# How the low parts of the up weights are made in a one-core decoder-layer kernel

## The chip, the core and the metric

The kernel runs on one core of a Trainium2 chip, as one program from its first load to its last store. The metric is the device time of one execution in microseconds (us), and less is better. Beside the time there is a profile of one execution: which instruction ran on which engine, from when to when, and what the DMA queues moved. The names of the engines in it are PE for the matrix unit (TensorE; PEld is its loading of weights), DVE for VectorE, ACT for ScalarE, POOL for GpSimd and SP for SyncE; a "q" behind a name (SPq) is that engine's sequencer, which issues DMAs.

## What is computed

One decoder layer for 256 tokens of width 2048, in float32. Its first half mixes tokens (pooling, attention over latents, attention over a memory); its second half, on which the change bears, is a gated feed-forward network with 5632 inner columns:

```python
def conv_glu_ffn(h, w_gate, w_up, conv_w, conv_b, w_down):
    S = h.shape[1]
    g = h @ w_gate
    gp = jnp.pad(g, ((0, 0), (CONV_WIDTH - 1, 0), (0, 0)))
    gc = conv_b
    for j in range(CONV_WIDTH):
        gc = gc + conv_w[j] * gp[:, j:j + S]
    return (jax.nn.silu(gc) * (h @ w_up)) @ w_down
```

## The kernel before

**Two parts of every number.** The matrix unit is fed in a shorter form of float32 (F32R). To keep the precision, every operand is split: the high part is the number rounded to that form, and the low part is the number minus its high part. A product is then high weight by both parts of the activation, plus low weight by the high part of the activation. Activations lie as 512 columns: 256 high, then 256 low. So `gemm_t` issues for each 128 x 128 weight tile one matmul of 512 columns with the high part (line 104) and one of 256 columns with the low part (line 107). All activations of the feed-forward are kept in SBUF; only weights are streamed.

**How weights come in.** `load_w` (line 78) takes a 1 MiB block of weights (128 partitions by 2048 numbers) from memory into one of three `wr` tiles, with a DMA on SP's queue (line 81). `split_w` (line 84) works on half of such a block, 1024 columns: ScalarE copies it, rounded, into a `wh` tile (line 90), and VectorE subtracts that from the raw half into a `wl` tile (line 91). There are three `wh` and three `wl` tiles. Thus a `wh` tile can be written again when the eight matmuls of line 104 that read it are done, a `wl` tile when the eight of line 107 are done, and a `wr` tile can be loaded again when both halves have been copied and subtracted.

**The loop around the change.** The feed-forward first runs 44 times over blocks of 128 inner columns (line 631). One pass loads a block of gate weights and a block of up weights, and multiplies each with all 16 tiles of `h2`: four half blocks in a row on the matrix unit, here called G0, G1 (gate) and U0, U1 (up). Each half is eight matmuls of line 104 followed by eight of line 107. Behind the products stand small steps on ScalarE and VectorE: `scaled` (lines 623 to 629) for gate and up, the convolution (lines 640 and 642), the silu (line 643), their product (line 645) and the split of the result into `aT` (lines 128 and 129). Then 16 passes over the down weights follow (line 648), with the same `load_w` and `gemm_t`. The pool `fp` that holds `aT` and the small tiles of this stage is opened behind the mixing stage and takes the place of that stage's tiles (lines 617 to 621).

**What sets the order.** The kernel is written as a sequence of tile operations. A scheduler orders them for each engine by their place in the program and by when it reckons them ready, and it adds every wait. Each engine then executes its own list strictly in that order, so an instruction that waits holds up all those behind it on its engine. On ScalarE the copies of line 90 run three halves ahead of the matrix unit, and between them stand the small steps of the pass before.

GpSimd has no part in the feed-forward before the change; SP issues the weight loads and the stores of the output.

Of the kernel before, what the change touches and what calls it, by code (L numbers as in the profile page):

```python
# [18 lines left out]
P = 128  # L19
# [30 lines left out]
NVEC = _o  # L50
# per-token tables: cos | sin (each NT x 32), rope gains of q | k (64 each), pool edge factors (4 x 16)
TAB = {"cos": (0, NT * 32), "sin": (64, NT * 32), "gq": (128, 64), "gk": (192, 64), "edge": (256, 64)}
# [4 lines left out]
def layer(ctx, tc, xT_d, memT_d, vec_d, tab_d, w_z_d, w_mqkr_d, w_q_d, w_kv_d, w_mem_d, w_pool_d, w_o_d,  # L57
# [26 lines left out]
    def split_w(raw, o, n, cut=HS):  # L84
        """high and low parts of raw[:, o:o + n]"""
        hi = stage.tile([P, HS], F32R, tag="wh", name=nm("wh"), bufs=3)
        lo = stage.tile([P, HS], F32R, tag="wl", name=nm("wl"), bufs=3)
        for c in range(0, n, cut):
            e = min(n, c + cut)
            nc.scalar.copy(hi[:, c:e], raw[:, o + c:o + e])  # L90
            nc.vector.tensor_tensor(lo[:, c:e], raw[:, o + c:o + e], hi[:, c:e].bitcast(F32), op=ALU.subtract)  # L91
        return hi, lo

    def gemm_t(ps, raw, o, act, ks, first=True, last=True):
        """ps[:, :256] + ps[:, 256:] (+)= W[ks].T @ act(ks); W columns on partitions, tokens free.
        Tile i of W is raw[:, o + i * 128:]; act(k) has the parts of the activations of tile k."""
        ks = list(ks)
        nk = HS // P
        for c in range(0, len(ks), nk):
            kc = ks[c:c + nk]  # L100
            hi, lo = split_w(raw, o + c * P, len(kc) * P)
            end = last and c + nk >= len(ks)
            for i, k in enumerate(kc):
                nc.tensor.matmul(ps[:, :2 * T], hi[:, i * P:(i + 1) * P], act(k), start=first and c + i == 0,  # L104
                                 stop=False, skip_group_check=True)
            for i, k in enumerate(kc):
                nc.tensor.matmul(ps[:, T:2 * T], lo[:, i * P:(i + 1) * P], act(k)[:, 0:T], start=False,  # L107
                                 stop=end and i == len(kc) - 1, skip_group_check=True)

    def gemm_n(pss, hi, lo, act, k0, first, last):  # L110
        """pss[tt][j] (+)= act[:, k0:, tile tt].T @ W[:, :, span j]; tokens on partitions. hi/lo: [P, k, n]"""
        nk, n = hi.shape[1], hi.shape[2]
# [12 lines left out]
    def split_act(dst, src, scale=None):  # L125
        """dst[:, :T], dst[:, T:] = high and low parts of src (times a per-partition scale)."""
        if scale is None:
            nc.scalar.copy(dst[:, 0:T], src)
            nc.vector.tensor_tensor(dst[:, T:2 * T], src, dst[:, 0:T].bitcast(F32), op=ALU.subtract)
        else:  # L130
            nc.scalar.activation(dst[:, 0:T], src, AF.Copy, scale=scale)  # L131
            nc.vector.scalar_tensor_tensor(dst[:, T:2 * T], src, scale, dst[:, 0:T].bitcast(F32),  # L132
                                           op0=ALU.mult, op1=ALU.subtract)

# [1 line left out]
    vec = const.tile([P, NVEC], F32, name="vec")  # L136
# [14 lines left out]

    # the tensor engine's clock is raised, and the activation tables are loaded, while the first loads are on their way
    warm = const.tile([P, 1], F32, name="warm")
# [5 lines left out]
    def rsqrt_(dst, src, scale):  # L159
        """dst = (src * scale + eps) ** -0.5"""  # L160
        nc.scalar.activation(dst, src, AF.Sqrt, bias=eps[:], scale=scale)
        nc.vector.reciprocal(dst, dst)
# [19 lines left out]
    class SumSq:  # L182
        """sum over tiles and partitions of squares, per token"""

# [18 lines left out]
    def col_sums(ps, src):  # L203
        """ps[:, tt] = sum over partitions of src[:, tile tt]"""
        for tt in range(NT):
            nc.tensor.matmul(ps[:, tt:tt + 1], src[:, tt * P:(tt + 1) * P], ones[:, 0:1], start=True, stop=True)

    def head_sq(dst, src):
        """dst[:, h] = sum over the last dim of src[:, h, :]^2"""
        sq = mp.tile([P, 512], F32, tag="hsq", name=nm("hsq"), bufs=2)  # L210
# [4 lines left out]
    def to_features(dst, src, tt, n, scale=None, eng=None):  # L215
        """dst[:, i, tile tt] = src[:, i * 128:].T (times a per-partition scale), i < n <= 4"""
        ps = ps_aux()
# [10 lines left out]

# [1 line left out]
    mg = big.tile([P, KD, 2 * T], F32R, tag="act", name="mg")  # L230
# [9 lines left out]

# [1 line left out]
    mv = mp.tile([P, NT, XH, XD], F32, name="mv")  # L242
# [54 lines left out]
    mem_kv(0)  # L297
# [1 line left out]
    tab = mp.tile([P, NTAB], F32, name="tab")  # L299
    nc.sync.dma_start(tab[:], tab_d)  # L300
    # combined gains of the two sides of a score, and gained rotation tables
    gqk = mp.tile([P, 2], F32, name="gqk")
# [16 lines left out]

# [1 line left out]
    xs = SumSq()  # L321
# [12 lines left out]

# [1 line left out]
    NH = 288  # L336
# [22 lines left out]

# [1 line left out]
    def softmax_pv(ps, spans, f, v_of, dst):  # L361
        """ps: scores of each query tile at spans, keys in tiles of P; dst gets the parts of the output's transpose"""
        p = mp.tile([P, 512], F32, tag="p", name=nm("p"), bufs=2)
# [9 lines left out]
        for i, (a, b) in enumerate(spans):  # L373
            nc.vector.tensor_scalar(p[:, a:b], p[:, a:b], st[:, 6 + i:7 + i], None, op0=ALU.mult)
        # turned: for each key tile, the query tiles that see it
        tp = ps_aux()
# [24 lines left out]
    def half_add(dst, ps):  # L401
        """dst = ps[:, :T] + ps[:, T:]"""
        t = mp.tile([P, T], F32, tag="hadd", name=nm("hadd"), bufs=3)
        nc.scalar.copy(t[:], ps[:, 0:T])
        nc.vector.tensor_tensor(dst, t[:], ps[:, T:2 * T], op=ALU.add)

# [1 line left out]
    zl = mp.tile([P, 6, 2 * T], F32R, name="zl")  # L408
# [16 lines left out]

    # scale of the normalised latents, per token: s = rx * (rx^2 mean(z^2) + eps)^-0.5
    sl, sl2 = sm(4), sm(4)
# [10 lines left out]

# [1 line left out]
    zp = mp.tile([P, 4, T], F32, name="zp")  # L440
# [6 lines left out]

# [1 line left out]
    def pool_mix():  # L449
# [16 lines left out]

# [1 line left out]
    qkv = big.tile([P, 32, T], F32, tag="act", name="qkv")  # L468
# [6 lines left out]
    def rotate(dst, src, s, tt, nh):  # L475
        """dst = rotated src [P, nh, 64] with the gained tables of side s"""
        x1, x2 = src[:, :, 0:32], src[:, :, 32:64]
# [29 lines left out]

# [1 line left out]
    # keys are scaled by f_k = ((s_kv^2 |kn|^2 + rx^2 |kr|^2) / QK + eps)^-0.5 and turned  # L509
    sskr, fk, fkn, fkr = sm(NT), sm(NT * H), sm(NT * H), sm(NT * H)  # L510
# [30 lines left out]

# [1 line left out]
    pool_in(0)  # L543
# [8 lines left out]
    q_up(1)  # L552
    # f_q = s_q (s_q^2 mean + eps)^-0.5 / sqrt(QK), applied as the softmax scale
    fq = sm(NT * H)
# [15 lines left out]

# [1 line left out]
    def mla(h):  # L572
# [10 lines left out]
    def out_half(i, m):  # L583
        """x (+)= the part i of the output projection, for the pair of feature tiles m, m + 1"""
        raw = load_w(w_o_d[i][m // 2], STG)
# [13 lines left out]

# [1 line left out]
    h2 = big.tile([P, KD, 2 * T], F32R, tag="act", name="h2")  # L601
# [16 lines left out]

# [1 line left out]
    fp = ctx.enter_context(tc.tile_pool(name="ffn", bufs=1))  # L620
    aT = fp.tile([P, KF, 2 * T], F32R, name="aT")

    def scaled(ps, tag):
        """(ps[:, :T] + ps[:, T:]) * rstd"""
        t = fp.tile([P, T], F32, tag=tag, name=nm(tag), bufs=2)
# [5 lines left out]
    for f in range(KF):  # L631
# [4 lines left out]
        psu = ps_main()  # L636
        gemm_t(psu, raw, 0, lambda k: h2[:, k, :], range(KD))
        g = scaled(psg, "g")
# [21 lines left out]
def _pack(**i):  # L660
# [3 lines left out]
    def cols(w):  # L664
        """[k*128, m*128] -> [m, 128, k*128]: one block of columns per tile, rows on partitions"""
        k, m = w.shape[0] // P, w.shape[1] // P
        return np.ascontiguousarray(w.reshape(k, P, m, P).transpose(2, 1, 0, 3)).reshape(m, P, k * P)

    def rows(w, nk):
        """[k*128, n] -> [k/nk, 128, nk*n]: nk row tiles per block"""  # L670
        k, n = w.shape[0] // P, w.shape[1]
# [67 lines left out]
```

## Time and profile before

| | us |
|---|---|
| median of 3 runs | 1044.78 |
| lowest and highest of them | 1044.51 and 1045.87 |
| span of the profiled execution, first to last instruction | 1043.6 |
| of it: PE busy | 1034.8 |
| DVE busy | 708.8 |
| ACT busy | 542.5 |
| POOL busy | 1.5 |

The profiled execution has no time of its own beside its span; the runs lie 0.9 to 2.3 us above that span, which is what an execution has around it and from run to run. An engine's busy time is the sum of the durations of its instructions; it doesn't tell whether the engine set the time. That is read from a stage: which wait ends last there.

### The profile page before, as it was taken

What the parts mean: (1) busy time and instruction counts of PE and PEld (TensorE: products, weight loads), DVE (VectorE), ACT (ScalarE), POOL (GpSimd) and SP (SyncE); (2) the same over time, 40 slices, a digit from 0 to 9 for tenths busy, and PEclk for the clock granted to TensorE, in tenths of its full rate; (3) what the DMA queues carried; (4) which work ended last, traced back from release to release, by engine and by line L of the source; (5) the groups of instructions that cost most, each with busy time, mean ns of one, the idle gap of its engine ahead of it and who ended that gap; (6) DMA issues with size and microseconds to landing.
All of it is one profiled execution on the core that took longest, in us unless ns stands there. A gap on an engine that the chain in (4) does not pass through costs nothing.

```text
span 1043.6 us, 14921 instructions
## 1 busy us (share of the span) xinstructions
PE 1034.8 (99%) x5852; PEld 897.2 (86%) x5852; DVE 708.8 (68%) x1141; ACT 542.5 (52%) x828; POOL 1.5 (0%) x10
## 2 busy tenths in 40 slices
PE   8999999999999999999999999999999999999998
PEld 6798888778888888888888888888888888888887
DVE  6967689766887777777777777777776554454453
ACT  7847666544666555555455455455454343333342
POOL 0000000000000000000000000000000000000000
PEclk9999999999999999999999999999999999999999
DMA  8555444333555555545555455555555665665661
GB/s 334 206 185 197 159 162 172 121 122 121 184 180 202 179 185 202 180 184 202 180 184 202 181 183 202 182 183 200 184 181 180 202 194 185 211 196 181 223 197 46
DMA packets 31030, 191.83 MB, mean 184 GB/s; under 512 B 3440, under 2 KB 6000, under 8 KB 10864
## 3 DMA queue, kind: packets, MB, share of 16 engines
q1 hardware_dynamic: 30672, 190.49, 52.7%
q8 instruction: 46, 0.75, 0.3%
q10 hardware_dynamic: 288, 0.38, 0.1%
q14 instruction: 24, 0.20, 0.0%
HBM read 188.77 MB, written 2.10 MB: 183 GB/s over the span
## 4 chain that ended last, share of the span: by engine, by line
PE 98%; DMA 1%; ACT 0%; DVE 0%; SPq 0%; issue 0%
PE psm L104 56%; PE psm L107 29%; PE psm L123 3%; PE psm L121 3%; PE psm L122 3%; PE psa L578 1%; PE psa L219 1%; DMA wr<-in_w_mem 1%; PE psa L385 1%; PE psa L577 1%; PE psa L380 1%; PE psa L393 0%; PE psa L386 0%; PE psa L580 0%; DVE wl L91 0%; ACT wh L90 0%
## 5 line engine op out<-in xcount | busy, mean ns | idle before, releaser
L91 DVE TENSOR_TENSOR wl<-wr,wh 128x1024 fp32r<-128x1024 f32 (+2 forms) x368 | 431.6, 1174 | 270.6 <-ACT wh L90 237.1
L90 ACT CAST wh<-wr 128x1024 fp32r<-128x1024 f32 (+2 forms) x368 | 371.2, 1009 | 438.3 <-PE psm L104 350.4
L104 PE MATMUL psm<-h,wh 128*128 128x512 f32 x1408 | 352.7, 392 | 0.0
L104 PEld LDWEIGHTS psm<-h,wh 128*128 128x128 f32 x1408 | 253.3, 189 | 45.5 <-DVE h L132 0.3
L107 PEld LDWEIGHTS psm<-h,wl 128*128 128x128 f32 x1408 | 192.1, 190 | 13.7
L107 PE MATMUL psm<-h,wl 128*128 128x256 f32 x1408 | 196.5, 282 | 0.0
L104 PE MATMUL psm<-aT,wh 128*128 128x512 f32 x704 | 177.9, 393 | 0.0
L104 PEld LDWEIGHTS psm<-aT,wh 128*128 128x128 f32 x704 | 125.9, 189 | 22.2
L107 PEld LDWEIGHTS psm<-aT,wl 128*128 128x128 f32 x704 | 97.0, 190 | 7.7
L107 PE MATMUL psm<-aT,wl 128*128 128x256 f32 x704 | 99.3, 282 | 0.0
L104 PE MATMUL psm<-cat,wh 128*128 128x512 f32 x192 | 52.0, 398 | 0.0
L642 DVE SCALAR_TENSOR_TENSOR gc<-g,vec,gc 128x255 f32<-128x255 f32 x88 | 42.2, 480 | 1.5
L104 PE MATMUL psm<-xg,wh 128*128 128x512 f32 x160 | 43.0, 401 | 0.0
L104 PEld LDWEIGHTS psm<-cat,wh 128*128 128x128 f32 x192 | 33.5, 189 | 4.9
L104 PEld LDWEIGHTS psm<-xg,wh 128*128 128x128 f32 x160 | 28.7, 189 | 4.9
L107 PEld LDWEIGHTS psm<-cat,wl 128*128 128x128 f32 x192 | 27.3, 190 | 2.6
L121 PE MATMUL psm<-wh,mg 128*128 128x512 f32 x64 | 25.1, 399 | 3.2 <-ACT mg L131 3.1
L107 PE MATMUL psm<-cat,wl 128*128 128x256 f32 x192 | 28.1, 282 | 0.0
L640 ACT ACTIVATE gc<-g,vec 128x256 f32<-128x256 f32 x44 | 26.3, 597 | 0.0
L123 PE MATMUL psm<-wl,mg 128*128 128x512 f32 x64 | 24.7, 396 | 0.9 <-DVE wl L91 0.9
L122 PE MATMUL psm<-wh,mg 128*128 128x512 f32 x64 | 25.3, 395 | 0.1
L107 PE MATMUL psm<-xg,wl 128*128 128x256 f32 x160 | 24.7, 289 | 0.0
(173 smaller groups left out, 840.0 us busy)
## 6 DMA issues: line engine op xcount, KB each, us to landing
wr<-in_w_g SPq DMA_DIRECT2D x44, 1024.0 KB, 4.9
wr<-in_w_u SPq DMA_DIRECT2D x44, 1024.0 KB, 4.8
wr<-in_w_dn SPq DMA_DIRECT2D x32, 1024.0 KB, 5.1
wr<-in_w_o SPq DMA_DIRECT2D x16, 1024.0 KB, 4.8
wr<-in_w_dn SPq DMA_DIRECT2D x16, 768.0 KB, 4.2
wr<-in_w_z SPq DMA_DIRECT2D x10, 1024.0 KB, 4.8
wr<-in_w_mqkr SPq DMA_DIRECT2D x8, 576.0 KB, 3.8
wr<-in_w_mem SPq DMA_DIRECT2D x4, 1024.0 KB, 7.2
```

The lines of the kernel that those rows point to most:

```text
L90: nc.scalar.copy(hi[:, c:e], raw[:, o + c:o + e])
L91: nc.vector.tensor_tensor(lo[:, c:e], raw[:, o + c:o + e], hi[:, c:e].bitcast(F32), op=ALU.subtract)
L104: nc.tensor.matmul(ps[:, :2 * T], hi[:, i * P:(i + 1) * P], act(k), start=first and c + i == 0, stop=False, skip_group_check=True)
L107: nc.tensor.matmul(ps[:, T:2 * T], lo[:, i * P:(i + 1) * P], act(k)[:, 0:T], start=False, stop=end and i == len(kc) - 1, skip_group_check= ...
L121: nc.tensor.matmul(ps, xh, hi[:, i, o], start=first and i == 0, stop=False)
L122: nc.tensor.matmul(ps, xl, hi[:, i, o], start=False, stop=False)
L123: nc.tensor.matmul(ps, xh, lo[:, i, o], start=False, stop=last and i == nk - 1)
L219: nc.tensor.transpose(ps[:, i * P:(i + 1) * P], src[:, i * P:(i + 1) * P], identf[:])
L380: nc.tensor.transpose(tp[:, x * P:(x + 1) * P], p[:, a + k * P:a + (k + 1) * P], identf[:])
L385: nc.tensor.matmul(o[:, 0:T], v_of(0), pT[:, 0:T], start=True, stop=False, skip_group_check=True)
L640: nc.scalar.activation(gc[:], g[:], AF.Identity, bias=v("conv_b", f), scale=v("cw2", f))
L642: nc.vector.scalar_tensor_tensor(gc[:, d:T], g[:, 0:T - d], v(w, f), gc[:, d:T], op0=ALU.mult, op1=ALU.add)
```

## The change

In the 44 up products alone, the low parts no longer come from VectorE. ScalarE writes the negated, rounded weights into a new tile `wd` (two of them, in the pool `fp`), and a DMA on GpSimd's queue adds the same weights from memory to that tile. ScalarE makes the high part with a copy as before, behind the negation. The raw block is still loaded by SP, since both ScalarE steps read it. The gate, down and all earlier products keep `split_w`. (The diff also takes out comments, which are left out here.)

```diff
+    def split_w_dma(raw, o, n, src):
+        hi = stage.tile([P, HS], F32R, tag="wh", name=nm("wh"), bufs=3)
+        lo = fp.tile([P, HS], F32R, tag="wd", name=nm("wd"), bufs=2)
+        nc.scalar.activation(lo[:, :n], raw[:, o:o + n], AF.Copy, scale=-1.0)
+        nc.gpsimd.dma_start(lo[:, :n], src[:, o:o + n], accum_op=ALU.add)
+        nc.scalar.copy(hi[:, :n], raw[:, o:o + n])
+        return hi, lo
 
-    def gemm_t(ps, raw, o, act, ks, first=True, last=True):
+    def gemm_t(ps, raw, o, act, ks, first=True, last=True, src=None):
...
-            hi, lo = split_w(raw, o + c * P, len(kc) * P)
+            if src is None:
+                hi, lo = split_w(raw, o + c * P, len(kc) * P)
+            else:
+                hi, lo = split_w_dma(raw, o + c * P, len(kc) * P, src)
...
-        gemm_t(psu, raw, 0, lambda k: h2[:, k, :], range(KD))
+        gemm_t(psu, raw, 0, lambda k: h2[:, k, :], range(KD), src=w_u_d[f])
```

## The prediction

> **What bounds the kernel now.** First the page: the busy times, and the chain of work that ended last.
>
> ```profile
> span 1043.6 us, 14921 instructions
> PE 1034.8 (99%) x5852; PEld 897.2 (86%) x5852; DVE 708.8 (68%) x1141; ACT 542.5 (52%) x828; POOL 1.5 (0%) x10
> ...
> PE 98%; DMA 1%; ACT 0%; DVE 0%; SPq 0%; issue 0%
> ```
>
> The chain is the matrix unit nearly from end to end. VectorE's 68% counts for nothing unless the matrix unit waits for it, so the next view is the table of windows: two passes of the gate/up loop, 100 us of that loop, 100 us of the down products, and a stretch at the start.
>
> ```profile
> core 0: us, PE busy (x) PEld busy (x) DVE busy (x) ACT busy (x) POOL busy (x), PEclk, DMA share, GB/s
> 10.00:20.00 10.00, 8.68 (x34) 6.00 (x35) 9.36 (x17) 10.00 (x18) 0.00 (x0) 1.00 1.03 410
> ...
> 405.70:416.87 11.17, 11.17 (x66) 9.83 (x65) 8.05 (x13) 5.85 (x10) 0.00 (x0) 1.00 0.53 190
> 416.87:428.05 11.18, 11.18 (x67) 9.84 (x66) 8.06 (x13) 5.86 (x10) 0.00 (x0) 1.00 0.53 189
> ...
> 400.00:500.00 100.00, 100.00 (x574) 87.94 (x573) 72.27 (x108) 52.14 (x82) 0.00 (x0) 1.00 0.53 187
> 900.00:1000.00 100.00, 100.00 (x574) 87.82 (x574) 50.11 (x54) 38.81 (x40) 0.00 (x0) 1.00 0.60 195
> ```
>
> A pass takes 11.17 us, the matrix unit has no gap in it, and its granted clock is full. The last two rows matter most: 574 matmuls in 100 us where VectorE is busy 72.27, and 574 where it is busy 50.11. The pace of the matrix unit does not depend on VectorE's load, so VectorE time set free is worth nothing here. With clock and number of matmuls unchanged, the change can hardly win; the question is whether the new way of making a low part is ready in time.
>
> **Part 1: the work moved between engines.** From the groups by line, over the whole gate/up stage:
>
> ```profile
> L91 DVE TENSOR_TENSOR wl<-wr,wh 128x1024 fp32r<-128x1024 f32 x179 | 219.3, 1225 | 131.2 <-ACT wh L90 123.6 <-ACT g L626 7.5
> ...
> L90 ACT CAST wh<-wr 128x1024 fp32r<-128x1024 f32 x179 | 187.9, 1050 | 234.6 <-PE psm L104 180.6 <-issue 54.0
> ```
>
> A pass loses two subtractions of 1.225 us on VectorE: 88 in all, 107.8 us, and VectorE falls from 8.05 to 5.60 us a pass. ScalarE gains two negations of the shape of the copy, 1.05 us each: 92.4 us in all, and 5.85 becomes 7.95 of 11.17 us a pass. Neither is a bound; this costs and gains 0, hidden behind the matmuls. ScalarE would have to gain 5.3 us a pass to come out.
>
> **Part 2: the time that the new transfer has.** Now the timeline. At 408.69 ScalarE reads the finished gate product, so the half that starts at 408.49 is U0, then U1 (411.29), G0 (414.08), G1, and the next U0 at 419.67.
>
> ```profile
> 408.49 2.00 PE L104 MATMUL psm<-h,wh 128*128 128x512 f32 x8
> 408.69 0.37 ACT L626 COPY g<-psm 128x256 f32<-128x256 f32 x1
> ...
> 410.33 1.11 PE L107 MATMUL psm<-h,wl 128*128 128x256 f32 x8
> ...
> 410.59 1.05 ACT L90 CAST wh<-wr 128x1024 fp32r<-128x1024 f32 x1 [1.52 <-PE psm L104]
> ...
> 411.29 2.00 PE L104 MATMUL psm<-h,wh 128*128 128x512 f32 x8
> 411.54 0.60 ACT L640 ACTIVATE gc<-g,vec 128x256 f32<-128x256 f32 x1
> ...
> 412.92 0.33 SPq L81 DMA_DIRECT2D wr<-in_w_u  x1
> ...
> 413.37 1.05 ACT L90 CAST wh<-wr 128x1024 fp32r<-128x1024 f32 x1 [1.23 <-issue]
> ...
> 414.08 2.00 PE L104 MATMUL psm<-h,wh 128*128 128x512 f32 x8
> ...
> 418.46 0.33 SPq L81 DMA_DIRECT2D wr<-in_w_g  x1
> ...
> 419.67 2.00 PE L104 MATMUL psm<-h,wh 128*128 128x512 f32 x8
> ...
> 421.51 1.12 PE L107 MATMUL psm<-h,wl 128*128 128x256 f32 x8
> ...
> 424.30 1.12 PE L107 MATMUL psm<-h,wl 128*128 128x256 f32 x8
> ```
>
> With two `wd` tiles and two up halves a pass, U0 always uses the same tile. Its negation waits until line 107 of the U0 before is done, at 411.29. ScalarE's copy from 410.59 ends at 411.64; the negation then takes until 412.69, and GpSimd can ask for the transfer. The low part is first read at 421.51. **The cover is 421.51 - 412.69 = 8.8 us.** For U1 the tile is free at 414.08, the copy at 413.37 ends at 414.42, the negation at 415.47, and the reading starts at 424.30: again 8.8 us. The negation is a new wait in ScalarE's list: behind it stand the copy for the next `wh` and the small steps of lines 640 and 643. Those have slack (the copy at 413.37 serves a half that starts at 419.67, over 5 us after its end), so this wait costs 0 while transfers are in time. SP's loads gain a little: a block of up weights is free after ScalarE's last copy, one subtraction (1.2 us) sooner. GpSimd's queue is otherwise empty here.
>
> If a transfer takes L from the request, a pass lasts from line 107's end to the next: 1.40 us to the negation's end, L, and 0.95 us of matmuls, so max(11.17, L + 2.37).
>
> **Part 3: what the transfer costs.** The trace of before has no adding DMA. What it has are plain ones (KB each, us to landing; the last row is from the crowded start), and the two strips of the window 405.70 to 416.87, in 40 slices of 0.28 us.
>
> ```profile
> wr<-in_w_u SPq DMA_DIRECT2D x44, 1024.0 KB, 4.8
> wr<-in_w_mqkr SPq DMA_DIRECT2D x8, 576.0 KB, 3.8
> ...
> wr<-in_w_mem SPq DMA_DIRECT2D x7, 512.0 KB, 8.9
> ```
> ```profile
> DMA  6000000009072999999940000000092639899999
> GB/s 293 0 0 0 0 0 0 0 0 205 0 235 117 411 440 440 469 440 440 469 147 0 0 0 0 0 0 0 0 205 59 147 147 469 352 440 411 411 411 440
> ```
>
> The engines carry two loads a pass in bursts and are idle between. One MiB costs them 1.0486 MB / 410 GB/s = 2.56 us by the saturated row 10:20, or 0.53 x 11.17 / 2 = 2.96 us by the share in the loop; I take the middle, 2.76.
>
> The adding transfer of a half must fetch 512 KB of weights and, to add to it, the 512 KB that stands in the tile. Bounds: **at best** it costs the engines what a plain 512 KB does, 1.38 us, and lands after some 3.7 us (the 576 KB row, a little less). Then a pass holds 2 x 2.76 + 2 x 1.38 = 8.3 us of DMA in 11.17: hidden, 0. **At worst** nothing overlaps and it costs three or four such passes of 512 KB: 5.5 + 6 x 1.38 = 13.8, or 5.5 + 8 x 1.38 = 16.5 us a pass, so 2.6 or 5.4 us over 11.17, times 44: 116 or 236 us. The 8.9 us row shows how long 512 KB can take in a crowd; two such one behind the other in one queue, 17.8 us, would be 6.6 over, 292 us. **I take double**, as for two streams of 512 KB each: 2.76 us a half, so 11.04 us of DMA in 11.17. Such a budget only just fits, and it does not fit in this order: U0's transfer, asked for at 412.7, moves from about 413.9 (the load asked for at 407.29 moves from 408.5) beside the load of 412.92; both are done 5.5 us later, at 419.4. U1's waits behind it in GpSimd's queue, then shares the engines with the load asked for at 417.3 to 418.5, and ends at 419.4 + 5.5 = 424.9; with 0.7 for the receipt (bytes end at 411.4 for a landing at 407.29 + 4.8 = 412.1) it lands at 425.6, 1.3 us after 424.30. A pass that is stretched gives the engines more room, so the lateness that stays lies between 0.1 (the budget alone, with ordinary small losses) and 1.3 us; I take 0.9, nearer to the upper end since the burst repeats every pass. 44 x 0.9 = 40 us.
>
> The Trainium skill, "DMA: Bandwidth & Descriptors", § Issuing engines are not separate DMA queues, says that DMAs started by GpSimd end on the same 16 engines as SP's and interleave with them. By it the sharing above holds; if GpSimd's queue had engines of its own, the sum would be 0. The page shows other queues as shares of the same 16 engines, but GpSimd issued none before.
>
> **Part 4: the entry.** The new tiles lie where the mixing stage had its tiles. If that place comes free only with the stage's last reader, the first negations start late:
>
> ```profile
> 306.43 0.42 DVE L612 TENSOR_TENSOR xacc<-xacc,sq 128x256 f32<-128x256 f32 x1
> ...
> 309.77 1.11 PE L107 MATMUL psm<-h,wl 128*128 128x256 f32 x8
> ```
>
> 306.85 + 1.05 + 3.7 to 8.8 us is 311.6 to 316.7 against the first use at 309.77: 2 to 7 us once; if the place was free earlier, 0. I take 0, and keep 7 in the range.
>
> **Sum.** 1043.6 span + 40 = 1083.6; with the 1.2 us by which the median of the runs stands above the span, 1085.
>
> **Rivals.**
> *Double cost, DMA-bound* (forecast): 0.1 to 2 us a pass, 1049 to 1133.
> *Hidden* (the other side): the added transfer costs little more than a plain one and lands within the 8.8 us of cover. Then nothing is late, and the time is 1044.8, or to 1052 with the entry. It decides at L = 8.8 us and at an engine cost of (11.17 - 5.52) / 2 = 2.8 us a half. For it: 47% of the engines' time is idle, and 8.8 us is more than twice 3.7; against it: two streams for one.
> The skill's page named above, § Anatomy of one DMA, fits a GpSimd DMA as 2.0 us plus bytes at 436 GB/s: an estimate of 3.2 us for 512 KB, by which the time is 1044.8. No run here shows it for an adding DMA.
> *Heavy*: the add costs three passes or more, or serial landings: 1133 to 1340, by the sums of part 3. For it: nothing in the trace says that reading, adding and writing overlap; against it: plain loads do stream at 410 GB/s.
> *ScalarE's order*: negations in its list hold up the copies of `wh`. A pass with 7.95 us of ScalarE work and 5 us of lead would not show it: 0; with the lead lost, both negations of each pass would show, 92 us.
> *It doesn't do what it says*: if the adding still went by VectorE or the load of raw blocks were gone, VectorE's count or SP's would show it; the diff says neither.
> *Faster*: only if the matrix unit itself ran quicker; the two rows of 574 speak against it.
>
> **How the numbers follow.** Forecast 0.38, heavy 0.30, hidden 0.29, faster 0.03. The time predicted is the forecast's 1085; its own range is 1049 to 1133. The range for 8 in 10 must take in the hidden case (from 1043.5) and the lower part of the heavy one: 1250 leaves out its upper two fifths (0.12) and the faster case, 0.15 in all. About 0.2% (2.1 us) is what a measurement can tell from no change. Faster 0.03, same 0.29, slower 0.68.
>
> **What would show it.** Part 1: 88 fewer instructions of line 91, VectorE near 5.6 us and ScalarE near 8 us a pass. Parts 2 and 3: gaps on the matrix unit before line 107 of U0 and U1, released by the adding DMA, and a DMA share near 1 (forecast) or far below (then a latency, not the engines, is the bound); POOL's issues with a landing above 8.8 us. Hidden: no gaps, landing under 8.8 us. Part 4: one gap near 310 us. I am wrong if a landing above 8.8 us leaves the pass at 11.17, or if the passes stretch while the landings stay short: then the wait sits in ScalarE's or SP's list.

## The result, and the profile after

The changed kernel takes 1157.86 us (median of 4 runs, 1155.19 to 1159.66) against 1044.91 us before: 1.1079 times, with a 95% interval of 1.1063 to 1.1094. That is slower, as forecast, by 113 us and not by 40.

The page of the changed kernel: span, busy times, DMA queues, and the chain that ended last.

```profile
span 1153.4 us, 15010 instructions
...
PE 1077.7 (93%) x5852; PEld 920.5 (80%) x5852; DVE 609.3 (53%) x1053; ACT 629.9 (55%) x916; POOL 77.6 (7%) x98
...
q1 hardware_dynamic: 30672, 190.49, 48.5%
q0 software_dynamic: 12672, 46.14, 21.9%
...
PE 67%; DMA 25%; ACT 5%; issue 2%; DVE 0%; SPq 0%; ACTq 0%; POOLq 0%
...
wd<-in_w_u POOLq DMA_DIRECT2D x88, 512.0 KB, 8.6
```

A quarter of the chain is now DMA, all but a little of it the adding transfer. VectorE lost 88 instructions and 99.5 us, ScalarE gained 88 and 87.4 us. Two different losses stand in the PE row. The span grew by 109.8 us. PE's idle time (span minus busy) grew from 8.8 to 75.7 us, by 66.9. But PE's busy time grew as well, by 42.9 us, with the same 5852 matmuls: they ran slower. The windows of the changed kernel show when (same columns as before the change):

```profile
340.00:800.00 460.00, 404.73 (x2114) 344.68 (x2112) 191.61 (x332) 259.50 (x365) 57.83 (x67) 0.93 0.86 227
363.61:389.87 26.26, 22.97 (x129) 19.61 (x129) 11.36 (x20) 15.75 (x22) 3.45 (x4) 1.00 0.97 254
405.00:800.00 395.00, 345.73 (x1792) 294.67 (x1792) 162.40 (x281) 220.17 (x309) 49.20 (x57) 0.92 0.85 224
```

From 363.61 to 389.87 two passes take 13.1 us each, the DMA engines are 97% busy, and the granted clock is full. From 405 on the clock is 0.92, and the engines are only 85% busy although the passes are longer. The timeline of the changed kernel shows two of U0's requests and one such stretch; line 119 is the old line 107, line 116 the old 104, and `wd` marks U0 and U1.

```profile
420.62 0.86 POOL L99 DMA_DIRECT2D wd<-in_w_u  x1 [8.33 <-PE psm L116]
...
449.76 0.86 POOL L99 DMA_DIRECT2D wd<-in_w_u  x1 [9.65 <-PE psm L116]
...
502.39 1.12 PE L119 MATMUL psm<-h,wd 128*128 128x256 f32 x8
...
505.18 1.12 PE L119 MATMUL psm<-h,wd 128*128 128x256 f32 x8
...
505.44 0.86 POOL L99 DMA_DIRECT2D wd<-in_w_u  x1 [8.78 <-PE psm L116]
...
508.31 0.86 POOL L99 DMA_DIRECT2D wd<-in_w_u  x1 [2.01 <-ACT wd L98]
...
514.14 1.22 PE L119 MATMUL psm<-h,wd 128*128 128x256 f32 x8 [0.42 <-DMA wd<-in_w_u]
...
520.57 2.08 PE L119 MATMUL psm<-h,wd 128*128 128x256 f32 x8 [3.37 <-DMA wd<-in_w_u]
```

U0's transfer, asked for at 505.44, is read at 514.14 with a wait of 0.42 us. U1's, asked for at 508.31, lets the matrix unit go on at 520.57: 12.3 us after the request, against a cover of 8.8, and a gap of 3.37 us. Behind that gap eight matmuls of line 119 take 2.08 us instead of 1.12: the granted clock is 0.50 from 520.57 to 522.44. Long gaps like this one stand before U1 in every second pass from 405 to 800 us, 2.8 to 3.5 us each. The pass before has no gap at all; gapless and gapped passes alternate. From the request of U0 at 420.62 to that two passes later at 449.76 it is 29.1 us, where two old passes were 22.3.

### The profile page after: what moved, and what is told of

Its sections match the earlier page's. It is cut to its first block, busy times and chain, and to the rows that moved or that the text cites. A ratio compares the mean times of both kernels' runs of the same rounds, so it can differ in the third digit from the quotient of the medians.

```text
span 1153.4 us, 15010 instructions
## 1 busy us (share of the span) xinstructions
PE 1077.7 (93%) x5852; PEld 920.5 (80%) x5852; DVE 609.3 (53%) x1053; ACT 629.9 (55%) x916; POOL 77.6 (7%) x98
## 3 DMA queue, kind: packets, MB, share of 16 engines
q1 hardware_dynamic: 30672, 190.49, 48.5%
q0 software_dynamic: 12672, 46.14, 21.9%
## 4 chain that ended last, share of the span: by engine, by line
PE 67%; DMA 25%; ACT 5%; issue 2%; DVE 0%; SPq 0%; ACTq 0%; POOLq 0%
PE psm L116 36%; DMA wd<-in_w_u 25%; PE psm L119 20%; PE psm L135 3%; PE psm L133 3%; PE psm L134 3%; ACT wd L98 2%; ACT wh L100 1%; PE psa L590 1%; PE psa L231 1%; ACT gc L655 1%; ACT u L638 1%; DMA wr<-in_w_mem 1%; PE psa L397 1%; PE psa L589 0%
## 5 line engine op out<-in xcount | busy, mean ns | idle before, releaser
L91 DVE TENSOR_TENSOR wl<-wr,wh 128x1024 fp32r<-128x1024 f32 (+2 forms) x280 | 323.9, 1159 | 268.5 <-ACT wh L90 242.5
L90 ACT CAST wh<-wr 128x1024 fp32r<-128x1024 f32 (+2 forms) x280 | 278.8, 996 | 337.2 <-PE psm L116 301.5
L116 PE MATMUL psm<-h,wh 128*128 128x512 f32 x1408 | 371.5, 408 | 0.0
L119 PE MATMUL psm<-h,wd 128*128 128x256 f32 x704 | 113.1, 308 | 68.3 <-DMA wd<-in_w_u 67.9
L119 PEld LDWEIGHTS psm<-h,wd 128*128 128x128 f32 x704 | 101.5, 208 | 90.2 <-DMA wd<-in_w_u 84.2
L99 POOL DMA_DIRECT2D wd<-in_w_u x88 | 76.1, 865 | 815.0 <-ACT wd L98 654.2
L100 ACT CAST wh<-wr 128x1024 fp32r<-128x1024 f32 x88 | 92.2, 1048 | 54.0 <-PE psm L116 52.8
L119 PEld LDWEIGHTS psm<-h,wl 128*128 128x128 f32 x704 | 98.7, 195 | 7.6
L119 PE MATMUL psm<-h,wl 128*128 128x256 f32 x704 | 100.2, 286 | 0.0
L98 ACT ACTIVATE wd<-wr 128x1024 fp32r<-128x1024 f32 x88 | 92.8, 1055 | 2.7 <-PE psm L119 2.5
```

What stands on the lines that cost most here:

```text
L98: nc.scalar.activation(lo[:, :n], raw[:, o:o + n], AF.Copy, scale=-1.0)
L99: nc.gpsimd.dma_start(lo[:, :n], src[:, o:o + n], accum_op=ALU.add)
L100: nc.scalar.copy(hi[:, :n], raw[:, o:o + n])
```

## The experiments

All of them are edits of the changed kernel unless "the kernel before" is named. "Before" was timed beside each group, at 1045.1 to 1045.2 us.

**Is it the adding?** (plain_no_add)

```diff
-        nc.gpsimd.dma_start(lo[:, :n], src[:, o:o + n], accum_op=ALU.add)
+        nc.gpsimd.dma_start(lo[:, :n], src[:, o:o + n])
```

> The 88 transfers of GpSimd's queue are plain ones of the same 512 KB: nothing is added, the low part of the up weights is left out (the tile holds the weights themselves). Issues, waits, queue and bytes landed stay as they are. Two streams on the 16 engines as the cause: an issue costs the engines about 1.5 us instead of 2.87, a pass holds 2 x 3.0 + 2 x 1.5 = 9.0 us of DMA in 11.17, landings under 8.8 us, no gaps: 1044 to 1048 us. GpSimd's queue, its 0.86 us issue or its fixed latency as the cause: still 1140 to 1160 us.

1050.87 us, 1.0058 (1.0043 to 1.0073). The page of this run, its queue of GpSimd:

```profile
span 1050.1 us, 15010 instructions
...
q0 software_dynamic: 12672, 46.14, 12.8%
```

Nothing is added here, so the low part is left out. Queue, packets and waits are the same (only GpSimd's issue falls from 0.86 to 0.53 us), and nearly the whole loss is gone. What a transfer costs the 16 engines is share times span over 88: 12.8% of 1050.1 is 1.53 us for the plain one; in the changed kernel 21.9% of 1153.4 is 2.87 us. So adding costs 1.9 times the plain transfer. The median landing falls from 8.6 to 5.5 us. The 5.6 us that are left are a little more than was expected (1048 us at most). The matrix unit waits for `wd` only twice in this run, 0.75 us at 310.28 and 3.55 us at 316.86, for the first two transfers; this entry is taken up below.

**Is it ScalarE's new work?** (negate_dve_add)

```diff
-        nc.gpsimd.dma_start(lo[:, :n], src[:, o:o + n], accum_op=ALU.add)
+        nc.vector.tensor_tensor(lo[:, :n], raw[:, o:o + n], lo[:, :n].bitcast(F32), op=ALU.add)
```

> The negation on ScalarE stays where it is, and VectorE adds the raw half to it in place of the DMA. The added ScalarE work and its waits as a cause: some of the 113 us stay, up to 92 us: 1060 to 1137 us. Transfers as the only cause: 1044 to 1047 us, with ScalarE near 8 us a pass.

1044.97 us, 0.9999 (0.9990 to 1.0008). The busy times of this run:

```profile
PE 1035.4 (99%) x5852; PEld 898.8 (86%) x5852; DVE 700.8 (67%) x1141; ACT 631.0 (60%) x916; POOL 1.5 (0%) x10
```

ScalarE is busy 631.0 us there, against 629.9 in the changed kernel, and it costs nothing. The negations and their place in ScalarE's list are excluded.

**Half as many transfers** (one_half_dma), and the same **from the second pass on** (one_half_late)

```diff
-            if src is None:
+            if src is None or c == 0:
```
```diff
-        gemm_t(psu, raw, 0, lambda k: h2[:, k, :], range(KD), src=w_u_d[f])
+        gemm_t(psu, raw, 0, lambda k: h2[:, k, :], range(KD), src=w_u_d[f] if f > 0 else None)
```

> Only U1 gets its low part by the DMA, U0 by VectorE as before the change: 44 adding transfers instead of 88. Two streams on the engines as the cause: 2 x 3.0 + 2.9 = 8.9 us of DMA a pass in 11.17, the transfer lands within its cover (which is the same 8.8 us and more, since each of the two tiles now has two passes): 1044 to 1050 us. A latency of each transfer by itself as the cause: about half of the loss, 1090 to 1105 us.

> As one_half_dma, but the first pass makes all low parts on VectorE; the DMA begins with the second pass. If the 4.8 us of one_half_dma are the late start of the first transfer at the entry to the stage, they go: 1044 to 1046.5 us. If they are small losses over the 44 passes, 1049 to 1050 us stay.

one_half_dma takes 1050.03 us, 1.0046 (1.0029 to 1.0063); one_half_late 1045.44 us, 1.0001 (0.9991 to 1.0011). With one adding transfer a pass the median landing is 6.4 us and nothing waits in the loop. The rest is one event, in the timeline of one_half_dma at the entry to the stage:

```profile
316.09 2.04 PE L119 MATMUL psm<-h,wd 128*128 128x256 f32 x8 [3.02 <-DMA wd<-in_w_u]
317.94 3.61 PE L116 MATMUL psm<-h,wh 128*128 128x512 f32 x8
```

A wait of 3.02 us for the first transfer, and behind it matmuls at half pace (3.61 for 2.00 us). With the first pass left to VectorE it is gone. So the entry costs about 5 us once; in the changed kernel it is there too, as waits of 2.12 and 1.35 us at 311.72 and 317.65.

**Filling the gap** (filler_6, filler_3)

```diff
+            if src is not None and c > 0:
+                fill = ps_aux()
+                for i in range(6):
+                    nc.tensor.matmul(fill[:, :2 * T], hi[:, i * P:(i + 1) * P], act(kc[i]), start=True, stop=True)
             for i, k in enumerate(kc):
                 nc.tensor.matmul(ps[:, T:2 * T], lo[:, i * P:(i + 1) * P], act(k)[:, 0:T], start=False,
```

(filler_3 has `range(3)`.)

> The changed kernel with six more matmuls of 512 columns in each U1 between line 116 and line 119, into a bank that nothing reads: 6 x 0.23 = 1.4 us more work a pass, 61 us in all. If a large part of the loss comes from the halved clock after a long gap of the matrix unit, the shorter gap keeps the clock up and the pass at about 13.0 us as in the stretch 363 to 390 us of the changed kernel: 1105 to 1135 us, faster than 1158 though it does more. If the clock has no part in it and only DMA sets the pass: 1158 us, the work vanishing in the gaps, or up to 1220 us where passes without a gap grow.

> As filler_6 with three added matmuls, 0.7 us a pass. wd_three and filler_6, which have little else in common, both end at 1115 us with the engines busy 95% of the stage: read as the floor that the engines' work sets, 12.6 us a pass. If that floor and the clock are all, three fillers that keep the long gaps away give about 1115 us again; if they don't keep them away, up to 1158 us. If instead filler_6 was just its own work on top of the kernel before (1044.8 + 61 + 5 at the entry), three give 1080 us.

filler_6 takes 1115.77 us, 1.0690 (1.0651 to 1.0728); filler_3 takes 1108.45 us, 1.0605 (1.0573 to 1.0637). Both do more than the changed kernel and are 42 and 49 us faster than it. The windows of filler_3 over the loop, then those of filler_6:

```profile
340.00:800.00 460.00, 445.89 (x2489) 383.24 (x2488) 214.31 (x371) 290.59 (x408) 63.87 (x74) 1.00 0.96 255
```
```profile
340.00:800.00 460.00, 459.01 (x2556) 398.85 (x2555) 211.09 (x366) 289.21 (x403) 63.02 (x73) 1.00 0.94 251
```

The clock is full all through, and the DMA engines are 96 and 94% busy where they were 86%. The last theory in the expectation of filler_3, 1080 us, falls: with three fillers the matrix unit still waits 14 of the 460 us for adding transfers, beside engines at 96%. With six it is busy 459.01 of 460 us, so there its own added work sets the time. The timeline of filler_3 has gaps before line 119's matmuls of U1 (line 123 there) of 1.29 us and less between 400 and 600 us, and no slow matmuls behind them:

```profile
429.29 1.13 PE L123 MATMUL psm<-h,wd 128*128 128x256 f32 x8
434.23 1.21 PE L123 MATMUL psm<-h,wd 128*128 128x256 f32 x8 [1.29 <-DMA wd<-in_w_u]
...
454.57 1.11 PE L123 MATMUL psm<-h,wd 128*128 128x256 f32 x8
459.10 1.22 PE L123 MATMUL psm<-h,wd 128*128 128x256 f32 x8 [0.90 <-DMA wd<-in_w_u]
```

**More cover** (wd_three)

```diff
-        lo = fp.tile([P, HS], F32R, tag="wd", name=nm("wd"), bufs=2)
+        lo = fp.tile([P, HS], F32R, tag="wd", name=nm("wd"), bufs=3)
```

> Three tiles wd instead of two (and one tile o instead of two, which only the stores of the down products use). A negation can start half a pass sooner, so a transfer may take up to 14.4 us. If the sum of the engines' work is what remains, about 11.9 us a pass against 11.17, with no long gaps and so no halved clock: 44 x 0.75 = 33 us and some 5 at the entry: 1075 to 1095 us. If the time of each transfer alone was the cause: 1045 to 1050 us. If a transfer has to wait for something else, such as the raw blocks: near 1158 us.

1114.81 us, 1.0667 (1.0647 to 1.0688): 43 us better than two tiles, but 20 us above what was expected. The windows of wd_three over the loop tell why:

```profile
340.00:800.00 460.00, 425.45 (x2330) 366.85 (x2329) 207.57 (x364) 278.60 (x401) 63.01 (x73) 0.97 0.94 249
```

The engines are at 94%; over the whole loop they don't reach more than some 96% in any of these kernels, so the floor that they set seems to lie higher than their bare work. Half a pass more for a transfer takes most of the long gaps away and cannot lower that floor. Nor can the third tile give its whole half pass: ScalarE's negations now wait 131.3 us in all for the raw block of up weights, and not at all for it in the changed kernel. How much of the 20 us is this wait isn't shown.

**Is an adding transfer two plain ones?** (plain_twice)

```diff
-        nc.gpsimd.dma_start(lo[:, :n], src[:, o:o + n], accum_op=ALU.add)
+        aside = fp.tile([P, HS], F32, tag="aside", name=nm("aside"), bufs=1)
+        nc.gpsimd.dma_start(aside[:, :n], src[:, o:o + n])
+        nc.gpsimd.dma_start(lo[:, :n], src[:, o:o + n])
```

> In place of each adding transfer two plain ones of the same 512 KB on GpSimd's queue: one into a tile that nothing reads, then one into wd (again nothing is added, the low part is left out; one tile o). If an adding transfer is for the engines two plain streams: about 3 us of engine time a half, 12 us a pass, and a time like that of the changed kernel, 1100 to 1170 us. If adding costs by something else, such as a dependence of the write on the read: clearly less than that, 1050 to 1090 us.

1232.7 us, 1.1794 (1.1775 to 1.1814): outside what either theory gave, and its time settles nothing. Each transfer into the one tile `aside` waits until the one before has landed (5.8 us at the median), and the transfer into `wd` stands behind it in GpSimd's queue. That serial wait is the edit's own; one line of the waits of plain_twice shows it (total, times, longest):

```profile
POOL aside L100 <- DMA aside<-in_w_u: 409.3, 82, 7.0
```

What can be used is the engines' time: q0 is busy for 22.3% of 1231.3 us with 176 plain transfers, 1.56 us each. Two are 3.1 us, against 2.87 for an adding one.

**Gaps without DMA.** Two kernels meant to do this, gap_long and gap_short, delayed the low part of U1 in the kernel before by a chain of small steps (core of the edit; three additions or one):

```diff
+                zero = fp.tile([P, 1], F32, tag="zero", name=nm("zero"), bufs=2)
+                nc.scalar.activation(zero[:], tick[:, 0:1], AF.Copy, scale=0.0)
+                for _ in range(gap):
+                    nc.vector.tensor_scalar(lo[:], lo[:].bitcast(F32), zero[:], None, op0=ALU.add)
```

> The kernel before, no DMA added. In each U1, between line 104 and line 107, the low part waits for a small matmul, a ScalarE step and three VectorE additions of zero to the low tile: a gap of some 3 us on the matrix unit in every pass. If the clock halves after such a gap, PE busy time rises too: the time is 1044.8 + 44 x gap + 1 to 2 us a pass, with a mean clock below 0.95. If not, PE busy stays at 1035 + 44 x 0.12 and the clock at 1.0.

> The same with one addition of zero instead of three, so a gap of 1 to 1.7 us. In the changed kernel the gaps of 1.6 us left the clock at 1.0: PE busy stays at about 1040 us here and the time is 1044.8 + 44 x gap, near 1100 us. If short gaps halve the clock too, it is 50 us more.

They gave 1064.1 and 1060.93 us (one run each), with the clock at 1.0: no gap arose, since the scheduler drew matmuls of the next half in front of the waiting ones. They tell nothing of gaps. So the next two, again from the kernel before, hold the first tile of `h2`, which every pass begins with (six additions in hold_long, one in hold_short):

```diff
+        zero = fp.tile([P, 1], F32, tag="zero", name=nm("zero"), bufs=2)
+        nc.scalar.activation(zero[:], psu[:, T:T + 1], AF.Copy, scale=0.0)
+        for _ in range(6):
+            nc.vector.tensor_scalar(h2[:, 0, :], h2[:, 0, :].bitcast(F32), zero[:], None, op0=ALU.add)
         g = scaled(psg, "g")
```

> The same with six additions instead of one: a gap of 3 to 4.5 us in every pass, as long as the long gaps of the changed kernel, without any DMA in it. Clock theory: windows of half clock appear after the gaps, PE busy rises by 1 to 1.7 us for each of them (40 to 75 us), mean clock 0.90 to 0.96, time 1044.8 + 44 x gap + that rise. If the halved clock of the changed kernel has another cause (the load on the memories, say), the clock stays at 1.0 and PE busy at 1035 us.

> The kernel before, no DMA added. Behind U1 of every pass a ScalarE step and one VectorE addition of zero to the first tile of h2 stand between the passes, which the first matmul of the next pass waits for: a true gap on the matrix unit of 1 to 1.7 us a pass. Clock theory: gaps of that length leave the clock at 1.0, PE busy stays at 1035 us, time 1044.8 + 44 x gap, 1090 to 1120 us.

One run each: 1373.51 and 1153.27 us. The timeline of hold_long, then that of hold_short: the first matmuls of a pass, with the gap in front of them.

```profile
507.78 3.75 PE L104 MATMUL psm<-h,wh 128*128 128x512 f32 x8 [5.42 <-DVE h L641]
511.34 1.84 PE L107 MATMUL psm<-h,wl 128*128 128x256 f32 x8
513.02 2.00 PE L104 MATMUL psm<-h,wh 128*128 128x512 f32 x8
```
```profile
479.65 3.54 PE L104 MATMUL psm<-h,wh 128*128 128x512 f32 x8 [1.89 <-DVE h L641]
494.54 2.11 PE L104 MATMUL psm<-h,wh 128*128 128x512 f32 x8 [1.89 <-DVE h L641]
507.87 2.11 PE L104 MATMUL psm<-h,wh 128*128 128x512 f32 x8 [1.89 <-DVE h L641]
521.19 2.12 PE L104 MATMUL psm<-h,wh 128*128 128x512 f32 x8 [1.89 <-DVE h L641]
534.53 3.69 PE L104 MATMUL psm<-h,wh 128*128 128x512 f32 x8 [1.89 <-DVE h L641]
...
602.75 3.68 PE L104 MATMUL psm<-h,wh 128*128 128x512 f32 x8 [1.89 <-DVE h L641]
```

The windows of hold_long over the loop, then those of hold_short:

```profile
340.00:800.00 460.00, 329.62 (x1585) 282.06 (x1584) 251.32 (x437) 147.77 (x245) 0.00 (x0) 0.86 0.32 112
```
```profile
340.00:800.00 460.00, 395.48 (x2161) 340.68 (x2160) 288.30 (x439) 203.18 (x339) 0.00 (x0) 0.98 0.44 154
```

With no added DMA at all, a gap of 5.42 us (longer than was planned) is followed by slow matmuls: 3.75 and 1.84 us instead of 2.00 and 1.11, with a granted clock of 0.50 from 507.78 to 511.34. It is so in all eleven passes that begin between 400 and 620 us. PE's busy time in hold_long is 1128.5 us, 93.7 more than before and more than the 40 to 75 that were expected. So long gaps by themselves bring the clock down, and the gap costs twice: itself, and some 2.2 us of slower matmuls behind it (93.7 over 43 gaps).

The expectation of hold_short failed: a gap of 1.89 us is followed by slow matmuls in about one pass of five, the clock does not stay at 1.0, and PE is busy 1061.2 us, 26.4 more than before or 0.6 us a gap. The time is 1153.27 us and not 1090 to 1120.

## Why the prediction was right and wrong

*Bound and direction: right.* The matrix unit set the time, VectorE's freed time was worth nothing (one_half_late frees 49 us of it and ties), and the new transfers decide.

*Part 1, the engines' work: right.* negate_dve_add measures it at 0 with an interval of about 1 us to either side.

*Part 2, the cover of 8.8 us: right in kind.* Waits appear exactly on `wd`, and landings of 8.7 us (514.14) just fail while 12.3 us (520.57) fails by 3.4. The cover itself was a little shorter: U0's negation of 504.10 stands behind the step that was line 640 on ScalarE and ends 1.8 us after the tile is free (503.34), not 1.40, and GpSimd asks 0.3 us later, which the forecast had not counted. From the request at 505.44 the matrix unit could have gone on at 513.72, after 8.3 us.

*Part 3, double cost: right, and measured.* Taken 2.76 us a half, found 2.87; plain 1.53, taken 1.38. Two loads at 3.03 us (52.7% of 1043.6 us for 190.49 MB in the page of before) and two adding transfers make 11.8 us a pass; forecast 11.04. U1 as the late one, behind U0's transfer in one queue, was right as well.

*The term that was mis-sized: the lateness of 0.9 us a pass.* It came to (113 - 5) / 44 = 2.45 us, with 5 us for the entry taken off. Two things are in it.
First, the engines' floor. The forecast let the lateness lie between 0.1 and 1.3 us, with a budget that just fits. With the clock up, filler_3 ends 63 us over the kernel before: less 5 for the entry, 58 over 44 passes is 1.3 us a pass at best. (wd_three, with the clock at 0.97, and filler_6, which its added matmuls limit, end 70 over.) This is the upper end of the forecast's bounds. Most of it is that the work is 11.8 us and not 11.04, and that the engines are no more than 96% busy over the loop: 11.8 / 0.96 = 12.3 us, 1.1 over 11.17. Why they stop short of 100% isn't shown.
Second, and missing from the prediction: *what a late transfer does to the matrix unit.* "A pass that is stretched gives the engines more room" was the step that failed. The room came as a gap of 2.8 to 3.5 us in every second pass, the clock halved behind it, and the engines fell to 85% busy; as the timeline suggests, slow matmuls release `wd` late, and the next requests come late with them. That is the other 42 to 49 us: 1157.9 against 1108 to 1116 for three kernels that differ from the changed one in fillers or a tile. That gaps halve the clock is shown without DMA by hold_long; that kernels with fewer long gaps give back 42 to 49 us is shown by the fillers and by wd_three. How those 42 to 49 us divide between the halved clock and the uneven order of transfers stays open, since the fillers and the third tile change both at once. PE's busy time grew by 42.9 us in the changed kernel, which is about as much; but in wd_three 23.3 us of that growth are still there (1058.1), and it ends no later than filler_6.

*Part 4, the entry: taken 0, kept 2 to 7; measured about 5 us* (one_half_dma against one_half_late).

*Rivals.* "Heavy" gave a time of the right size by the wrong cause: an adding transfer does not cost three passes. "Hidden" was said to be decided at 2.8 us of engine time a half. The runs lie on either side of it, 1.53 us hidden and 2.87 not; no run tests the border itself. The fit of the Trainium skill ("DMA: Bandwidth & Descriptors", § Anatomy of one DMA), 3.2 us for 512 KB, is below even the plain transfer's 5.5 us beside the loads.

None of these kernels is faster than the kernel before; one_half_late and negate_dve_add tie with it.

## What to carry to other kernels

An adding DMA from memory is not free VectorE work: count it as two streams on the engines that also carry the loads, and put the sum of a pass, over the busy share that the engines reach (0.94 to 0.96 in the loops here), beside the pass. In a loop bound by the matrix unit, work taken off an engine that was not waited for is worth nothing, and a transfer that comes late now and then can cost more than its lateness. Where such waits can't be avoided, keep the gaps of the matrix unit short: gaps of 1.29 us and less in filler_3 had no slow matmuls behind them, one of 1.89 us cost 0.6 us of slower matmuls on average, one of 5.42 us cost 2.2. Here even matmuls whose result nothing reads paid, by 42 to 49 us, though the kernel before stays far ahead.

## What was not expected of the hardware

The matrix unit's granted clock fell after gaps as short as 1.89 us (hold_short), though only in about one of five, in a pattern that repeats over passes of 13.3 us: rows at 479.65, 534.53 and 602.75 are slow, those between are not. The nine slow rows of the run lie 54.9, 68.2 (six times) or 81.8 us apart. The Trainium skill, "TensorE: Matmul & The Clock Gate", § What's actually happening, describes a free-running window of 3413 ns over which the activity is judged; that fits a gap that counts only where it falls well in a window, and the three distances are 16.1, 20.0 and 24.0 such windows. The same page of the Trainium skill, § Why this matters for your kernels, warns of gaps above about 3 us; here 1.89 us was enough at times, and the measurement decides.

Issuing an adding transfer holds GpSimd for 0.86 us, a plain one of the same shape for 0.53 us.
